# One spread table for the head norm weights and sinks, accumulating transfers kept away from the merge transposes, and new places for side work, in a hybrid attention/MLP step

## The chip, the cores and the metric

The kernel runs on one core of a Trainium2 chip. The metric is the time of one execution on the device, in microseconds (us): the median of the runs before is 1329.82 us (three runs, 1328.12 to 1332.52). One execution was also taken with the hardware profiler; its trace gives start, duration and cause of waiting of each instruction.

A core has five engines that each run their own list of instructions in order and wait for each other by semaphores: TensorE (PE in the profile, with PEld for its weight loads), VectorE (DVE), ScalarE (ACT), GpSimd (POOL) and SyncE (SP), which here only issues transfers (DMAs).

## The reference, cut to what matters

One trunk layer of a diffusion backbone, for 128 context tokens (`x_prompt`) and 128 latent tokens (`x_sample`), width 2048, all in float32:

```python
sh1, sc1, g1, sh2, sc2, g2 = split(silu(cond) @ w_ada + b_ada, 6)
h = rms_norm(x, norm1_w) * (1 + sc1) + sh1
qa, ka, va, qb, kb, vb, ga, gb = split(h @ w_in)        # 2048 x 8704
qa, ka = rms_norm(qa, q_norm_a), rms_norm(ka, k_norm_a) # per head of 128
qb, kb = rms_norm(qb, q_norm_b), rms_norm(kb, k_norm_b)
oa = windowed attention, 8 heads, 2 kv heads, a learned sink logit sink_a per head
ob = neighbourhood attention, 8 heads, relative position bias
x = x + g1 * ((sigmoid(ga) * (oa @ w_br_a) + sigmoid(gb) * (ob @ w_br_b)) @ w_out)
h2 = rms_norm(x, norm2_w) * (1 + sc2) + sh2
x = x + g2 * (relu(h2 @ w_up) ** 2 @ w_down)            # 2048 x 8192 x 2048
```

Latent tokens also get a rotary embedding and attend to cached context keys. The new context keys and values are outputs as well.

## The kernel before, in words

**Weight steps.** The 256 tokens are the stationary side of the matmuls and the weights stream past them. All weights come as tiles of 128 x 1024 floats (512 KB, `raw`). A float32 product is made of three fast ones: a tile is split into a rounded high half `wH` and a rest `wL`, the tokens likewise (`hH`, `hL`), and PE adds wH·hH, wL·hH and wH·hL into `acc`. One tile is one *weight step*: a load issued by SP (L220), a copy to `wH` by ACT (L98), a subtraction `wL` = `raw` − `wH` by DVE (L246), and twelve matmuls (L296 to L298, or L414 to L416 in the first projection). There are 456 such steps: 0 to 71 the first part of the input projection (nine units q, k, v, taken in chunks of the depth), 72 to 135 the eight gate units, 136 to 167 the two branches (`w_br_a`, `w_br_b`, four column units each), 168 to 199 `w_out`, and 200 to 455 the MLP in pieces of an up part and a down part. The up part forms some products from sums of two tiles (`XH`, `XL`, `YB`, `FAST`).

**The low half by transfer.** For the steps in the list `LO_DMA` DVE does not subtract. ACT writes −wH into `wL` (L252), and POOL issues a transfer that adds the weight tile to it in memory (L253, `accum_op`). Nineteen steps are on the list, among them 163, the last tile of the fourth `w_br_a` unit.

**Order.** The order is written by hand. `run()` goes through the steps; for step i it first issues the loads due up to step i + RUN[i], then prepares `wH` and `wL` up to step i + LOOK[i], then the step's matmuls, then the side work hung on that step (`at`). Each of RUN and LOOK is a string with a digit for each step. A name with `_AT`, `POST`, `JOBS`, `T_PAIR`, `P_PAIR`, `P_UP`, `T_UP`, `DOTS` is a table of the step, or the distance in steps, at which a piece of side work stands. An engine takes its instructions in that order, so one that waits holds up all that stand behind it on the same engine.

**Side work that the prediction names.**
- *Constants* (`load_consts`, loaded at the place CONST_AT[0], near step 68): the rotary table, three head norm weights of 128 floats each spread over the 128 partitions, the sink logits spread in the same way, and the cached keys and values. They go through SP's queue among the weight tiles. `load_bias` (CONST_AT[1]) loads the position bias, which POOL then masks with eight selects (L643, L645).
- *Head norm* (`POST`): ACT squares (L664), POOL raises to −1/2 (L141, L142), ACT and DVE apply it (L675 to L688).
- *Dots* (L1388, `DOTS1`, `DOTS`, `DOTS2`): the other part of the modulation is made on DVE, as row sums of `w_ada` tiles (`aT`) with silu(cond) (`cB`), 128 x 1024 at a time; the result goes to `aT` or to `junk` by turns. The first part is made on PE in pairs (`ps_ada`, L313).
- *Merge* (`br_unit`): the merged columns of unit n must be transposed to become the stationary side of `w_out`. For n = 0 to 2 this is done in three steps: `part` (ACT copies the halves of each float to 16-bit planes `plm`), `flip` (SP issues one transposing transfer, `pTm`, L871) and `join` (ACT puts the planes together as `fTm`, and ACT and DVE split it into `m0H`/`m0L` and so on). M_AT gives the distance of the three from the end of the unit. Unit 3 is transposed by PE (`ps_T`, L848). `h2f` and `ps_h` (L1029, L1037) are the second norm.

Of the kernel before, what the change touches and what calls it, by code (L numbers as in the profile page):

```python
# [18 lines left out]
P = 128  # L19
D = 2048  # L20
KC = D // P
HD = 128
NH = 8
# [9 lines left out]
FB_DVE = 2  # L33
FB1 = 14
H_AT = 38
DOTS1 = [11, 15, 23, 28, 29, 31, 33, 34]
CHUNKS = [2, 2, 2, 4, 6]
NFAST = 8
FAST = {1: (0, 3, 7), 2: (0, 2, 4, 6, 7), 3: (0, 2, 3, 4, 7), 4: (0, 2, 4, 6, 7), 5: (0, 1, 3, 4, 7), 6: (0, 1, 4, 5, 7), 7: (0, 3, 4, 6, 7)}
SEED_AT = 3  # L40
KEEP = True
ROWS_AT = [8, 6, 3]
SEED1_AT = 2
SEED1 = "101111011111111111001100111011111111"
# [7 lines left out]
LOOK = "234335453022344432223322221123343443443222223775666676366646455654435553343455556665357644436452334433332233221321432244644644245355400233120425355623477665676447546554534564644667674253021316344751443634211245334554433356554223123421445424543633220000235565775443654553304536544534445434543233444323223545687654344342323322202410232434423542333435554555523324223333334435433334435442300123332434534633245342656444443412231330344475554454323213432233345544"  # L52
RUN = "649522021012233424433334222110112541121112232345556555534334554224554454565572101322134333222224454542222001333311333323442545661430123142722355655565555757423433576442014141257765376943474743254236564587423656644454665553123312233345542334335654105653231354445553432211112222432232322202344422121133432312342242430331200000222233345444243334543434963332212101334433643322111332122223312234344436665443012022332200131013374556744346778788775545334442222234"
# [8 lines left out]
PREP_IN = [6, 8]  # L62
DOTS = [33, 41, 44, 44, 47, 47, 48, 50, 52, 52, 52, 55, 57, 57, 57, 58, 62, 67, 70, 70, 73, 75, 82, 84, 84, 88, 90, 92, 93, 94, 95, 99, 99, 99, 103, 103, 105, 105, 108, 108, 111, 112, 114, 114, 115, 118, 119, 120, 121, 121, 124, 124, 125, 128, 129, 132, 132, 132, 132, 134, 136, 138, 140, 143, 143, 144, 149, 150, 151, 151, 152, 157, 157, 163, 165, 169, 171, 171, 173, 175, 176, 176, 178, 179, 179, 183, 183, 190]
DOTS2 = [222, 231, 232, 233, 235, 237, 238, 242, 245, 263, 265, 269, 275, 299, 301, 301, 302, 329, 331, 333, 333, 334, 358, 360, 362, 364, 366, 368, 383, 391, 392, 396]
STAT_AT = [-1, -1, 9, 17]
T_PAIR = [[8, 10], [6, 8], [8, 8], [8, 10], [10, 14], [8, 10], [11, 14]]
P_PAIR = [[6, 6], [2, 2], [1, 4], [4, 2], [3, 2], [5, 2], [4, 4]]
M_TE = (3,)
M_AT = [4, 6, 9]
FLIP = 1  # L70
P_UP = [3, 0]
T_UP = [6, 8]
COL = {"qA": 0, "kvA": 1024, "qB": 1536, "kB": 2560, "vB": 3584, "gA": 4608, "gB": 6656}


# [1 line left out]
def tile_hybrid_step(ctx: ExitStack, tc: tile.TileContext, a):  # L77
# [8 lines left out]
    act, dve, pe, pool, sync = nc.scalar, nc.vector, nc.tensor, nc.gpsimd, nc.sync  # L86
# [179 lines left out]

    by_dma = sorted(LO_DMA)

# [335 lines left out]
    def load_consts():  # L604
        rc = G("rope")[:, 0:256].rearrange("p (a b c) -> p a b c", a=2, b=4)
        sync.dma_start(rc.rearrange("p a b c -> p (a b c)"), a["rope"])
        k2 = G("k2")
        wb = k2[:, 512:896].rearrange("p (n d) -> p n d", n=3)
        for n, name in enumerate(("q_norm_a", "k_norm_a", "k_norm_b")):
            sync.dma_start(wb[:, n, :], a[name][0].partition_broadcast(P))  # L610
        dve.tensor_scalar(wb, wb, float(HD) ** 0.5, None, op0=OP.mult)
        dve.tensor_scalar(qkw, qkw, float(HD) ** 0.5, None, op0=OP.mult)
        K2["wb"] = {"kvA": wb[:, 1, :], "kB": wb[:, 2, :]}

        for n, name in enumerate(("qA", "kvA")):
# [12 lines left out]
        sync.dma_start(ca[:, 1], a["cache_a_v"][0, 0])  # L628
        kT, cbv = (G(n).rearrange("p (h d) -> p h d", h=NH) for n in ("kTcB", "cbv"))
        sync.dma_start(kT, a["cache_b_kT"])  # L630
        sync.dma_start(cbv, a["cache_b_v"][0, 0])
        K2["ca"], K2["kTcA"], K2["kTcB"], K2["cbv"] = ca, ca[:, 0], kT, cbv
# [874 lines left out]
def _layout(x):  # L1507

    def tiles(w, n=512):
        k, m = w.shape  # L1510
        return w.reshape(k // 256, 2, P, m // n, n).transpose(0, 3, 2, 1, 4).reshape(k // 256, m // n, P, 2 * n)

    out = {n: x[n] for n in ("x_prompt", "x_sample", "b_ada", "q_norm_a", "k_norm_a", "q_norm_b", "k_norm_b", "sink_a",
                             "cache_a_v", "cache_b_v")}
# [53 lines left out]
```

## Time and profile before

| | |
|---|---|
| median of 3 runs | 1329.82 us |
| profiled execution, its own time | 1329.58 us |
| its span, first to last instruction | 1327.8 us |
| POOL's 19 transfers L253, issue to landing | 5.2 / 8.3 / 17.3 us (min, median, max) |
| copy to wH on ACT, L98 | 392.4 us in 393, 1044 ns each |
| subtraction wL on DVE, L246 | 436.3 us in 368, 1223 ns each |
| dots on DVE, L1388 | 154.9 us in 128 (`aT`) and 154.2 us in 128 (`junk`) |
| bytes moved | 390.68 MB, mean 294 GB/s |

In the rows of a timeline the first number is the start in us from the span's start, the second the duration; then engine, line, operation, output<-input and how many instructions the row groups. A bracket gives the idle time before and what ended it. A row of stretches gives, for each engine, its busy time (and number of instructions), then the clock that TensorE was granted, the DMA share and the GB/s. Matmuls overlap: one starts about every 0.227 us and is shown as 0.39 us long.

### The profile page before, as it was taken

Reading aid. Unit: us, or ns where it says so; the run is one execution under the profiler, and the core shown is the slowest. Engines: PE = TensorE matmul, PEld = TensorE weight load, DVE = VectorE, ACT = ScalarE, POOL = GpSimd, SP = SyncE. Lnnn points to the kernel's source line nnn. Section 1 sums busy time; section 2 is a strip of 40 time slices with the busy share of each in tenths; the row PEclk is TensorE's granted clock in tenths of the full one; section 3 lists DMA queues with packets and bytes.
Section 4 is the critical chain, followed back from the end, with each engine's and each line's share of the span. In section 5 each row is a group of like instructions: output and inputs, shape, how many; then the busy total and the mean of one; then the engine's idle time right before and its main releaser. Section 6 shows DMA issues by size and latency. Waiting matters only on the chain.

```text
span 1327.8 us, 17958 instructions
## 1 busy us (share of the span) xinstructions
PE 1309.4 (99%) x6275; PEld 1062.4 (80%) x6276; DVE 1117.6 (84%) x1476; ACT 911.6 (69%) x1284; POOL 57.3 (4%) x65
## 2 busy tenths in 40 slices
PE   8999999999999999899999999999999999999998
PEld 4777788788787888787888888888888888888887
DVE  4557899988899999799769989898989999969654
ACT  5777665787755565555687777968768687786871
POOL 0000003321000000000000000000000000000000
PEclk9999999999999999999999999999999999999999
DMA  9999996967699999999677995879676786976592
GB/s 375 408 409 409 408 390 214 397 217 271 208 398 398 404 374 277 303 378 355 200 253 270 283 274 203 270 230 293 234 293 218 253 277 235 312 205 246 174 359 95
DMA packets 147963, 390.68 MB, mean 294 GB/s; under 512 B 51872, under 2 KB 53088, under 8 KB 147872
## 3 DMA queue, kind: packets, MB, share of 16 engines
q1 hardware_dynamic: 144448, 378.16, 78.9%
q0 software_dynamic: 3280, 11.29, 4.7%
q8 instruction: 49, 0.80, 0.2%
q14 instruction: 42, 0.34, 0.1%
q10 hardware_dynamic: 144, 0.08, 0.0%
HBM read 370.83 MB, written 8.70 MB: 286 GB/s over the span
## 4 chain that ended last, share of the span: by engine, by line
PE 82%; DMA 6%; DVE 5%; issue 3%; ACT 2%; SPq 0%; POOL 0%; DVEq 0%; ACTq 0%; POOLq 0%
PE acc L297 14%; PE acc L298 14%; PE acc L296 14%; PE Q L1165 6%; PE Q L1164 6%; PE Q L1166 6%; PE acc L414 4%; PE acc L416 4%; PE acc L415 4%; DVE wL L246 3%; DMA araw<-in_w_pair 2%; PE ps_ada L313 2%; DMA wL<-in_w_br_a 1%; ACT wH L98 1%; DVE junk L1388 1%
## 5 line engine op out<-in xcount | busy, mean ns | idle before, releaser
L246 DVE TENSOR_TENSOR wL<-raw,wH 128x1024 fp32r<-128x1024 f32 x368 | 436.3, 1223 | 104.7 <-ACT wH L98 103.6
L98 ACT ACTIVATE wH<-raw 128x1024 fp32r<-128x1024 f32 (+1 forms) x393 | 392.4, 1044 | 50.8 <-DMA raw<-in_w_out 9.3
L1388 DVE SCALAR_TENSOR_TENSOR aT<-aT,cB 128x1024 f32<-128x1024 f32 x128 | 154.9, 1227 | 0.7
L1388 DVE SCALAR_TENSOR_TENSOR junk<-aT,cB 128x1024 bf16<-128x1024 f32 x128 | 154.2, 1221 | 0.4 <-ACT t L956 0.4
L414 PE MATMUL acc<-wH,hH 128*128 128x512 f32 x276 | 108.9, 394 | 0.0
L415 PE MATMUL acc<-wL,hH 128*128 128x512 f32 x276 | 107.6, 390 | 0.0
L416 PE MATMUL acc<-wH,hL 128*128 128x512 f32 x276 | 107.5, 390 | 0.0
L297 PE MATMUL acc<-wL,hH 128*128 128x512 f32 x256 | 100.0, 391 | 2.5 <-DVE wL L246 2.5
L296 PE MATMUL acc<-wH,hH 128*128 128x512 f32 x256 | 102.5, 400 | 0.0
L298 PE MATMUL acc<-wH,hL 128*128 128x512 f32 x256 | 99.9, 390 | 0.0
L98 ACT ACTIVATE uH<-raw 128x1024 fp32r<-128x1024 f32 x33 | 35.0, 1062 | 63.9 <-DVE raw L1226 62.1
L414 PEld LDWEIGHTS acc<-wH,hH 128*128 128x128 f32 x276 | 51.8, 188 | 13.2 <-issue 2.1
L416 PEld LDWEIGHTS acc<-wH,hL 128*128 128x128 f32 x276 | 51.8, 188 | 11.0
L415 PEld LDWEIGHTS acc<-wL,hH 128*128 128x128 f32 x276 | 51.8, 188 | 10.6 <-DVE wL L246 0.3
L297 PEld LDWEIGHTS acc<-wL,hH 128*128 128x128 f32 x256 | 48.2, 188 | 12.7 <-DVE wL L246 3.3
L296 PEld LDWEIGHTS acc<-wH,hH 128*128 128x128 f32 x256 | 48.1, 188 | 10.2 <-ACT prob L788 0.4
L298 PEld LDWEIGHTS acc<-wH,hL 128*128 128x128 f32 x256 | 48.1, 188 | 10.2
L98 ACT ACTIVATE tH<-t 128x1024 fp32r<-128x1024 f32 x33 | 35.0, 1060 | 29.9 <-DVE t L1219 26.3
L1229 DVE TENSOR_TENSOR uL<-raw,uH 128x1024 fp32r<-128x1024 f32 x33 | 40.4, 1225 | 1.2
L98 ACT ACTIVATE acc<-dsum 128x512 f32<-128x512 f32 x56 | 31.7, 590 | 13.7 <-DVE t L950 7.8
L98 ACT ACTIVATE fTa<-pTa 128x2048 uint16<-128x2048 uint16 x16 | 40.5, 2530 | 0.7 <-DMA pTa<-pla 0.7
L1228 DVE TENSOR_TENSOR tL<-t,tH 128x1024 fp32r<-128x1024 f32 x33 | 40.1, 1216 | 1.0 <-PE Z L1165 1.0
(644 smaller groups left out, 3200.7 us busy)
## 6 DMA issues: line engine op xcount, KB each, us to landing
raw<-in_w_in SPq DMA_DIRECT2D x133, 512.0 KB, 9.0
raw<-in_w_down SPq DMA_DIRECT2D x128, 512.0 KB, 6.3
raw<-in_w_upF SPq DMA_DIRECT2D x66, 512.0 KB, 4.8
araw<-in_w_pair SPq DMA_DIRECT2D x64, 512.0 KB, 10.2
aT<-in_w_adaT SPq DMA_DIRECT2D x64, 512.0 KB, 8.9
aT<-in_w_gT SPq DMA_DIRECT2D x64, 512.0 KB, 7.4
raw<-in_w_up SPq DMA_DIRECT2D x62, 512.0 KB, 5.2
raw<-in_w_out SPq DMA_DIRECT2D x32, 512.0 KB, 11.6
```

The source lines that it names most:

```text
L98: act.activation(out, in_, AF.Copy)
L246: dve.tensor_tensor(st["lo"], st["raw"], st["hi"].bitcast(F32), op=OP.subtract)
L296: pe.matmul(acc[tb], sh, wh[:, k, :], start=f, stop=False, skip_group_check=seeded)
L297: pe.matmul(acc[tb], sh, wl[:, k, :], start=False, stop=False, skip_group_check=seeded)
L298: pe.matmul(acc[tb], sl, wh[:, k, :], start=False, stop=l, skip_group_check=seeded)
L414: pe.matmul(acc[tb], sh, wh[:, k, :], start=opened[u] and k == 0, stop=False, skip_group_check=skip)
L415: pe.matmul(acc[tb], sh, wl[:, k, :], start=False, stop=False, skip_group_check=skip)
L416: pe.matmul(acc[tb], sl, wh[:, k, :], start=False, stop=last and k == 1, skip_group_check=skip)
L1164: pe.matmul(acc, stat[0], hi, start=f, stop=False)
L1165: pe.matmul(acc, stat[0], lo, start=False, stop=False)
L1166: pe.matmul(acc, stat[1], hi, start=False, stop=l)
L1388: dve.scalar_tensor_tensor(out, box["raw"], 1.0, cB[s, tag], op0=OP.mult, op1=OP.mult, accum_out=dst[:, s, fb:fb + 1])
```

## The change

The three head norm weights and the sinks are put into one array `heads` on the host (392 floats, repeated for 128 partitions, 200 KB) and come in one load in place of four. Steps 86 and 163 leave the LO_DMA list, so that DVE subtracts there, and 67, 330 and 363 join it, for which ACT and POOL do the work; an assertion keeps the list free of steps 148 to 173 (br0 is 136). M_AT starts the merge planes and their transposes earlier, and many entries of RUN, LOOK and the tables of side work are new. The changes in SEED1 leave the instructions as they were; FAST has as many fast products as before, in other places.

```diff
-DOTS1 = [11, 15, 23, 28, 29, 31, 33, 34]
+DOTS1 = [11, 17, 23, 28, 29, 31, 35, 35]
-FAST = {1: (0, 3, 7), 2: (0, 2, 4, 6, 7), 3: (0, 2, 3, 4, 7), 4: (0, 2, 4, 6, 7), 5: (0, 1, 3, 4, 7), 6: (0, 1, 4, 5, 7), 7: (0, 3, 4, 6, 7)}
+FAST = {1: (0, 5, 7), 2: (0, 2, 4, 6, 7), 3: (0, 2, 3, 4, 7), 4: (0, 2, 3, 4, 7), 5: (0, 1, 3, 4, 7), 6: (0, 1, 4, 5, 7), 7: (0, 3, 4, 6, 7)}
-BACK = 8
+BACK = 7
-GATE_BACK = 8
+GATE_BACK = 7
-LO_DMA = [86, 107, 129, 145, 163, 177, 184, 187, 189, 192, 236, 250, 254, 255, 297, 389, 392, 404, 436]
+LO_DMA = [67, 107, 129, 145, 177, 184, 187, 189, 192, 236, 250, 254, 255, 297, 330, 363, 389, 392, 404, 436]
-CONST_AT = [68, 64]
+CONST_AT = [68, 66]
-ADA_AT = [None, 4, 13, 18, 21, 38, 29]
+ADA_AT = [None, 4, 13, 18, 21, 38, 31]
-M_AT = [4, 6, 9]
+M_AT = [3, 4, 9]
...
@@ load_consts
         wb = k2[:, 512:896].rearrange("p (n d) -> p n d", n=3)
-        for n, name in enumerate(("q_norm_a", "k_norm_a", "k_norm_b")):
-            sync.dma_start(wb[:, n, :], a[name][0].partition_broadcast(P))
+        sync.dma_start(k2[:, 512:896 + NH], a["heads"])
...
-        sync.dma_start(sk[:, 0, :], a["sink_a"][0].partition_broadcast(P))
...
     br0 = len(wsteps)
+    assert not any(br0 + 12 <= j < br0 + 38 for j in LO_DMA)
...
@@ _layout
+    heads = np.concatenate([x[n].reshape(-1) for n in ("q_norm_a", "k_norm_a", "k_norm_b", "sink_a")])
+    out["heads"] = np.broadcast_to(heads, (P, 3 * HD + NH))
```

What this does to the order is seen best in three places. First SP's queue near step 68, where the constants stand among the weight tiles (the kernel before):

```order
L220 DMA raw<-in_w_in 128x1024 x3
L606 DMA rope<-in_rope 128x256
L610 DMA k_2276<-in_q_norm_a 128x128
L610 DMA k_2276<-in_k_norm_a 128x128
L610 DMA k_2276<-in_k_norm_b 128x128
L623 DMA k_2276<-in_sink_a 128x8
L627 DMA cacheA<-in_cache_a_kT 128x256
```

and the same place of the changed kernel, where the bias load stands too:

```order
L635 DMA bias<-in_rpb_qk 128x1024
L220 DMA raw<-in_w_in 128x1024 x2
L606 DMA rope<-in_rope 128x256
L609 DMA k_2277<-in_heads 128x392
L625 DMA cacheA<-in_cache_a_kT 128x256
```

Four small loads have become one, and the bias load has come closer to them, with two weight tiles between.

Second ACT's list around the second merge transpose (fTm is its result as ACT puts it together; L252 is the negated copy of step 163, L826 a gate's sigmoid), before:

```order
L98 ACTIVATE wH<-raw 128x1024
L98 ACTIVATE plm_5009<-g_gA_4509 128x1024 x2
L98 ACTIVATE wH<-raw 128x1024
L252 ACTIVATE wL<-wH 128x1024
L98 ACTIVATE wH<-raw 128x1024 x3
L826 ACTIVATE g_gB_4775<-g_gB_4775 128x1024
L98 ACTIVATE fTm_5112<-pTm_5059 128x2x1024
L98 ACTIVATE m1H<-fTm_5112 128x1024
L98 ACTIVATE wH<-raw 128x1024 x4
```

and of the changed kernel:

```order
L98 ACTIVATE wH<-raw 128x1024
L98 ACTIVATE plm_4987<-g_gA_4508 128x1024 x2
L98 ACTIVATE wH<-raw 128x1024 x5
L824 ACTIVATE g_gB_4791<-g_gB_4791 128x1024
L98 ACTIVATE fTm_5109<-pTm_5006 128x2x1024
L98 ACTIVATE m1H<-fTm_5109 128x1024
L98 ACTIVATE wH<-raw 128x1024 x3
```

The negated copy is gone, and the wH copy of one more step (165) stands ahead of fTm.

Third DVE's list ahead of the low half of step 181, around the first residual sum of `w_out` (t and x), before:

```order
L1388 SCALAR_TENSOR_TENSOR aT,half_4535<-aT,cB_3696 128x1024
L950 TENSOR_TENSOR t<-g_0_5177,acc 128x512 x2
L952 TENSOR_TENSOR x_0_4538<-x_0_4538,t 128x512 x2
L1388 SCALAR_TENSOR_TENSOR junk,half_4587<-aT,cB_3694 128x1024
L1388 SCALAR_TENSOR_TENSOR aT,half_4587<-aT,cB_3696 128x1024
L1388 SCALAR_TENSOR_TENSOR junk,half_4535<-aT,cB_3694 128x1024
L1388 SCALAR_TENSOR_TENSOR junk,half_4587<-aT,cB_3694 128x1024
L246 TENSOR_TENSOR wL<-raw,wH 128x1024 x3
```

and of the changed kernel:

```order
L1387 SCALAR_TENSOR_TENSOR aT,half_4542<-aT,cB_3693 128x1024
L1387 SCALAR_TENSOR_TENSOR junk,half_4590<-aT,cB_3691 128x1024
L1387 SCALAR_TENSOR_TENSOR junk,half_4542<-aT,cB_3691 128x1024
L949 TENSOR_TENSOR t<-g_0_5169,acc 128x512 x2
L951 TENSOR_TENSOR x_0_4545<-x_0_4545,t 128x512 x2
L1387 SCALAR_TENSOR_TENSOR aT,half_4590<-aT,cB_3693 128x1024
L1387 SCALAR_TENSOR_TENSOR aT,half_4542<-aT,cB_3693 128x1024
L1387 SCALAR_TENSOR_TENSOR junk,half_4590<-aT,cB_3691 128x1024
L1387 SCALAR_TENSOR_TENSOR aT,half_4590<-aT,cB_3693 128x1024
L1387 SCALAR_TENSOR_TENSOR junk,half_4542<-aT,cB_3691 128x1024
L1387 SCALAR_TENSOR_TENSOR junk,half_4590<-aT,cB_3691 128x1024
L246 TENSOR_TENSOR wL<-raw,wH 128x1024 x3
```

Both pieces begin right behind the low halves of steps 179 and 180, and the last row is that of 181 to 183. Five dots stood between; now there are nine, three ahead of the residual sum and six behind it. The other four stood ahead of steps 179 and 180 before.

More of the change, by code (lines that the diff above doesn't have):

```diff
@@ L43 @@
 SEED1_AT = 2
-SEED1 = "101111011111111111001100111011111111"
-BACK = 8
+SEED1 = "101111011101111111111100111011111111"
+BACK = 7
 AWAY = [('gA', 1), ('gB', 2), ('gB', 3), ('gA', 0), ('gB', 0), ('gA', 2)]
-GATE_BACK = 8
+GATE_BACK = 7
 DIRECT = (3,)
-LO_DMA = [86, 107, 129, 145, 163, 177, 184, 187, 189, 192, 236, 250, 254, 255, 297, 389, 392, 404, 436]
+LO_DMA = [67, 107, 129, 145, 177, 184, 187, 189, 192, 236, 250, 254, 255, 297, 330, 363, 389, 392, 404, 436]
 LO_AHEAD = 2
-LOOK = "234335453022344432223322221123343443443222223775666676366646455654435553343455556665357644436452334433332233221321432244644644245355400233120425355623477665676447546554534564644667674253021316344751443634211245334554433356554223123421445424543633220000235565775443654553304536544534445434543233444323223545687654344342323322202410232434423542333435554555523324223333334435433334435442300123332434534633245342656444443412231330344475554454323213432233345544"
@@ L53 @@
[L53 to L54 removed]
+LOOK = "003435353022344232233323121123244343443222223775666676366746456654545452243455556665357644436452334433332233221320432034644644155344400233121425465623477665686447335542534664644666674153010205332640443745321334123554433356554212012421444314543633220001335565775443654553305536544534445435654332334323223545687654344342323322202521343544423543433435554665523324323222434435433334434442302345532434534633245341556444443302331330343364454454323213543333345544"
@@ L55 @@
+RUN = "256423133014343646521012013111102542111112221345556555534335665335654454565472212333234333223323233542333112334422444423442545661440145364944455655565666867533433576442035252257754265833575723254358785687423556644454665563123311233345542334325655205653231354445674432201112222542232322202344422121144543323342242420331100000222233345333132224543334963223312101334433643322122432122223312234344436665332012133443310010012264557843225667688775546445663322234"
+CONST_AT = [68, 66]
 XL_DMA = []
-ADA_AT = [None, 4, 13, 18, 21, 38, 29]
+ADA_AT = [None, 4, 13, 18, 21, 38, 31]
@@ L61 @@
 T_AT = [4, 4]
[L62 to L67, printed above, removed]
+PREP_IN = [6, 7]
+DOTS = [33, 41, 44, 44, 47, 47, 48, 50, 52, 52, 52, 55, 57, 57, 57, 58, 62, 67, 70, 71, 73, 75, 82, 84, 84, 88, 90, 92, 93, 94, 95, 99, 99, 99, 103, 103, 105, 105, 108, 108, 111, 112, 114, 114, 115, 118, 119, 120, 121, 121, 124, 124, 126, 128, 129, 132, 132, 132, 132, 134, 136, 138, 140, 143, 143, 144, 149, 151, 151, 152, 157, 157, 162, 163, 165, 172, 173, 174, 174, 175, 176, 176, 178, 179, 179, 183, 183, 190]
+DOTS2 = [226, 230, 232, 233, 235, 237, 238, 242, 245, 263, 265, 269, 275, 299, 301, 301, 302, 329, 331, 333, 333, 334, 358, 360, 362, 364, 366, 368, 383, 391, 392, 396]
+STAT_AT = [-1, -1, 8, 17]
+T_PAIR = [[8, 9], [6, 8], [8, 9], [8, 10], [10, 14], [8, 10], [11, 14]]
+P_PAIR = [[4, 6], [2, 2], [1, 4], [6, 2], [4, 2], [5, 2], [4, 2]]
 M_TE = (3,)
-M_AT = [4, 6, 9]
+M_AT = [3, 4, 9]
 FLIP = 1
-P_UP = [3, 0]
-T_UP = [6, 8]
+P_UP = [2, 0]
+T_UP = [6, 11]
 COL = {"qA": 0, "kvA": 1024, "qB": 1536, "kB": 2560, "vB": 3584, "gA": 4608, "gB": 6656}
@@ L1511, in tiles @@
         return w.reshape(k // 256, 2, P, m // n, n).transpose(0, 3, 2, 1, 4).reshape(k // 256, m // n, P, 2 * n)
-    out = {n: x[n] for n in ("x_prompt", "x_sample", "b_ada", "q_norm_a", "k_norm_a", "q_norm_b", "k_norm_b", "sink_a",
-                             "cache_a_v", "cache_b_v")}
+    out = {n: x[n] for n in ("x_prompt", "x_sample", "cache_a_v", "cache_b_v")}
+    heads = np.concatenate([x[n].reshape(-1) for n in ("q_norm_a", "k_norm_a", "k_norm_b", "sink_a")])
+    out["heads"] = np.broadcast_to(heads, (P, 3 * HD + NH))
     for n in ("w_in", "w_br_a", "w_br_b", "w_out", "w_up", "w_down"):
```

## The prediction

> **What bounds the kernel now.** I read the busy shares of the page first, then the table of what each engine waited for, then the stretches around the waits.
>
> ```profile
> PE 1309.4 (99%) x6275; PEld 1062.4 (80%) x6276; DVE 1117.6 (84%) x1476; ACT 911.6 (69%) x1284; POOL 57.3 (4%) x65
> ```
>
> TensorE (PE) is busy for 99% of the span. The change leaves its matmuls as they are, so it can gain only where PE waits or runs slowly. The table of PE's waits has (us in total, times, longest):
>
> ```profile
> PE acc L297 <- DMA wL<-in_w_br_a: 2.8, 1, 2.8
> PE acc L297 <- DVE wL L246: 2.5, 2, 1.8
> ...
> PE acc L1002 <- DMA wL<-in_w_out: 1.0, 1, 1.0
> PE ps_T L848 <- DVE g_gA L903: 0.7, 1, 0.7
> PE ps_h L1037 <- DVE h2f L1029: 0.7, 1, 0.7
> ```
>
> These five rows are 7.7 us; the rest of the table lies in the first 42 us, whose loads the change leaves in order. The first row is one stall, and PE's timeline there shows a second loss behind it (start, duration):
>
> ```profile
> 534.89 0.39 PE L298 MATMUL acc<-wH,oLA 128*128 128x512 f32 x1
> 535.11 0.39 PE L296 MATMUL acc<-wH,oHA 128*128 128x512 f32 x1
> 538.26 0.50 PE L297 MATMUL acc<-wL,oHA 128*128 128x512 f32 x1 [2.76 <-DMA wL<-in_w_br_a]
> ...
> 539.12 0.63 PE L297 MATMUL acc<-wL,oHA 128*128 128x512 f32 x1
> ...
> 542.49 0.39 PE L296 MATMUL acc<-wH,oHB 128*128 128x512 f32 x1
> ```
>
> Before the stall a matmul starts every 0.22 us. From 539.12 to 542.49 eight starts take 3.37 us, 0.42 each: 8 x 0.20 = 1.6 us lost after the pause. So this place costs 2.8 + 1.6 = **4.4 us**.
>
> Its cause: step 163 has its low half wL made by an accumulating transfer that POOL issues, and SP's transpose of merge plane 1 is under way at that time.
>
> ```profile
> 518.30 7.96 SPq L871 DMA_TRANSPOSE pTm<-plm  x1
> ```
> ```profile
> 520.88 0.85 POOL L253 DMA_DIRECT2D wL<-in_w_br_a  x1 [48.24 <-DVE aT L1388]
> ```
>
> The summary of each tile gives the time from issue to landing (min/median/max), for all 19 accumulating transfers and then for the three transposes:
>
> ```profile
> DMA to landing us min/median/max: 5.2/8.3/17.3
> ```
> ```profile
> DMA to landing us min/median/max: 10.3/11.0/20.6
> ```
>
> The maxima are this pair: 520.88 + 17.3 = 538.2, where PE resumes, and 518.30 + 20.6 = 538.9, where ACT resumes below. While both are open nearly nothing moves, though the DMA engines are marked busy (last two columns: DMA share, GB/s):
>
> ```profile
> 525.00:530.00 5.00, 5.00 (x24) 4.14 (x23) 5.00 (x7) 0.00 (x0) 0.00 (x0) 1.00 1.37 66
> 530.00:535.00 5.00, 5.00 (x24) 4.15 (x23) 5.00 (x9) 0.00 (x0) 0.00 (x0) 1.00 1.08 72
> ```
>
> ACT and DVE wait for the same transpose, and behind ACT's wait stand the next steps' wH copies:
>
> ```profile
> 519.53 1.06 ACT L252 ACTIVATE wL<-wH 128x1024 fp32r<-128x1024 f32 x1
> ...
> 538.94 2.51 ACT L98 ACTIVATE fTm<-pTm 128x2048 uint16<-128x2048 uint16 x1 [14.55 <-DMA pTm<-plm]
> ...
> 542.44 3.89 ACT L98 ACTIVATE wH<-raw 128x1024 fp32r<-128x1024 f32 x4
> ```
> ```profile
> 542.57 1.22 DVE L102 TENSOR_TENSOR m1L<-fTm,m1H 128x1024 fp32r<-128x1024 f32 x1 [5.51 <-ACT m1H L98]
> 543.71 4.62 DVE L246 TENSOR_TENSOR wL<-raw,wH 128x1024 fp32r<-128x1024 f32 x4
> ```
>
> **The change, part by part.** (a) *Step 163 leaves the DMA list.* DVE gets a subtraction (4.62 / 4 = 1.16 us), ACT loses a copy of 1.06 us, POOL a transfer. The transpose should then take what the other two took, 10.3 to 11.0 us, and land near 529; ACT resumes some 9 us earlier. DVE's new 1.16 us come out of its 5.51 us of idle time, and the wL of 163 to 165 stand ahead of m1L now. I take the whole -4.4. The bounds are -4.4 and -3.0. The -3.0 is if the transpose still lands at 538.9: wL.166 ends two subtractions behind 542.57, at 544.9, and PE, which would want it three steps (36 x 0.227 = 8.2 us) behind 535.3, at 543.5, waits 1.4 us there.
>
> The Trainium skill speaks against this step: "DMA: Bandwidth & Descriptors", section "Rules for kernel authors", has "A transpose next to ordinary DMAs needs nothing". By that the transpose would be as late without the accumulation, and (a) would be its small end; the trace has 20.6 us beside the accumulation against 10.3 and 11.0 without, so I weigh it as the weaker.
>
> (b) *Merge planes one step earlier; the merge transpose no longer late.* The ps_T wait at 560 is for DVE's merge sums. DVE gains 5.51 - 1.16 = 4.35 us, PE 4.4, so it nearly stays; with the dots moved around it I take -0.3 (bounds -0.7 and 0).
>
> (c) *One load for norm weights and sinks.* Stretches before (DMA share, GB/s last):
>
> ```profile
> 227.00:232.00 5.00, 5.00 (x24) 4.14 (x23) 5.00 (x7) 1.20 (x2) 2.56 (x2) 1.00 0.15 33
> ...
> 236.00:240.00 4.00, 4.00 (x20) 3.30 (x19) 4.00 (x9) 3.33 (x11) 2.32 (x2) 1.00 1.03 406
> ```
>
> While the four broadcasts are served the queue moves 33 GB/s instead of 406, for about 5 us. One 200 KB load at 406 GB/s is 0.5 us (an estimate from that row), so the weights behind it land about 4.5 us earlier. Who waits for them:
>
> ```profile
> 241.96 1.06 ACT L98 ACTIVATE wH<-raw 128x1024 fp32r<-128x1024 f32 x1 [2.64 <-DMA raw<-in_w_in]
> 242.93 1.07 ACT L98 ACTIVATE u_vB<-acc 128x512 f32<-128x512 f32 x2
> ```
>
> That wait starts the chain to the 2.5 us row: ACT's squares, POOL's power, DVE's query block, two dots, then wL.76:
>
> ```profile
> 249.88 2.48 POOL L142 TENSOR_TENSOR rq<-rs,pw 128x8 f32<-128x8 f32 x1
> ```
> ```profile
> 252.39 0.69 DVE L676 TENSOR_TENSOR u_qA<-u_qA,rq 128x512 f32<-128x512 f32 x1 [0.41 <-POOL rq L142]
> ...
> 255.25 1.22 DVE L1388 SCALAR_TENSOR_TENSOR aT<-aT,cB 128x1024 f32<-128x1024 f32 x1
> ...
> 257.96 2.36 DVE L246 TENSOR_TENSOR wL<-raw,wH 128x1024 fp32r<-128x1024 f32 x2 [0.34 <-ACT wH L98]
> ```
> ```profile
> 259.24 0.51 PE L297 MATMUL acc<-wL,hH 128*128 128x512 f32 x1 [0.76 <-DVE wL L246]
> ...
> 266.76 0.51 PE L297 MATMUL acc<-wL,hH 128*128 128x512 f32 x1 [1.78 <-DVE wL L246]
> ```
>
> The 2.64 us go, but u_vB waits for PE's own sum, whose last matmul is
>
> ```profile
> 240.83 0.39 PE L416 MATMUL acc<-wH,hL 128*128 128x512 f32 x1
> ```
>
> and ends at 241.2. So the chain moves by 242.93 - 241.2 = 1.7 us at most; I take 1.4, since a wH copy can stand in the way. A dot (1.2 us, the 255.25 row) that stood before the query block now follows it, ahead of wL.76. Net: wL.76 some 0.6 us earlier, and the 0.76 nearly goes. At the second place DVE and PE both come 0.6 earlier, and 1.78 stays. I take **-0.6**; the bounds are -2.5 (all goes) and +1.2 (chain unmoved, dot added).
>
> (d) *Late w_out stalls (1.0 and some tenths).* DVE is the pacer there; two of its idle times wait for wH behind accumulating steps whose raw had just landed:
>
> ```profile
> 591.91 2.36 DVE L246 TENSOR_TENSOR wL<-raw,wH 128x1024 fp32r<-128x1024 f32 x2 [0.96 <-ACT wH L98]
> ...
> 598.32 2.36 DVE L246 TENSOR_TENSOR wL<-raw,wH 128x1024 fp32r<-128x1024 f32 x2 [0.61 <-ACT wH L98]
> ```
>
> With the transfer queue 9 us earlier behind the transpose and PE only 4.4, these 1.6 us go: **-1.0** (bounds -1.4; +1.2, if the added subtraction shows instead). (e) The ps_h wait of 0.7 grows as PE comes earlier than DVE: +0.4 (0 to +1.1).
>
> (f) *The rest*: dots, fast positions, pair 6, bias load, steps 67, 330 and 363 on the DMA list in place of 86 and 163, all move work inside stages where PE waits for nothing in the table. Nearest in margin is the block of step 252, where XL ends at 787.27 and PE takes it at 787.94:
>
> ```profile
> 786.05 1.22 DVE L1225 TENSOR_TENSOR XL<-raw,XH 128x1024 fp32r<-128x1024 f32 x1
> ```
> ```profile
> 787.94 0.39 PE L1165 MATMUL Q<-XL,h20H 128*128 128x512 f32 x1
> ```
>
> Until step 330 DVE carries one subtraction more (1.16 against this 0.67). DVE's earlier idle times hide it, so 0; without that cover +0.5.
>
> The sum: -4.4 - 0.3 - 0.6 - 1.0 + 0.4 = -5.9 on the profiled execution's 1329.58 us (span 1327.8 and 1.8 around it), 1323.7. That execution lies 0.24 under the median of 1329.82, so **1323.9**, by itself 1321.5 to 1325.5.
>
> **Rivals.**
> *B, the heads load frees both stalls at 259 and 267.* For it: the 1.78 is behind the same POOL power step. Against: the added dot. (c) is -2.5: 1322.0.
> *C, DVE eats the gain.* PE comes 4.4 us earlier into w_out, DVE 4.35 at most; if the subtraction of step 163 is not hidden, (d) is +1.2 rather than -1.0: 1326.1. For it: DVE is the pacer from 565 to 625.
> *T, the transpose is slow by itself.* (a) -3.0, (d) 0, DVE gaining about 1 us on 3: +1.9 at step 181; -3.0 + 1.9 - 0.3 - 0.6 = -2.0: 1327.8.
> *D, the single load is no faster than the broadcasts.* Then (c) is +1.2 and the time 1325.7. Against it: 33 GB/s at a share of 0.15 is a queue that waits, and rows of the raw loads run at 406. The Trainium skill ("DMA: Bandwidth & Descriptors", section "Specifications") puts the least transfer for line rate at 512 B, which the broadcast rows have already; by that alone nothing would be won, and the 33 GB/s row disagrees for this pattern.
> *A, slower: VectorE becomes the bound of the dense stage.* If DVE gains no time by 252, its timeline of before plus 1.16 less the 0.67 of margin sets the end: +0.5 on 1329.82, 1330.3. It decides once DVE regains less than 0.5 us of its idle time before 780. Against it stand the 5.51 us alone.
>
> **How the numbers follow.** The forecast 0.48, C 0.17, B 0.10, T 0.10, D 0.08, A 0.07. Predicted is the likeliest, 1323.9. The low end is every term's good bound but (a), near 1320.5; the high end takes in C, D, T and comes up to A, 1330.0. A measurement of this kernel can tell about 0.3% (4.0 us) from no change: faster is under 1325.8. That is the forecast, B, and a part of D and C: 0.72. Over 1333.8 lies only a case of A that is worse than priced: 0.04. The rest, 0.24, is the same.
>
> **What would show it.** (a): no wait for wL<-in_w_br_a, the pTm maximum near 11 us, no 0.42 us pitch near 540. (b), (e): the ps_T and ps_h rows. (c): GB/s near 400 within 2 us of the heads load, a wait of about 1.9 us for wL L246 near 265. (d): no L1002 row. Wrong it would be if the pTm maximum stays near 20 us, or if new rows for wL L246 appear behind 650.

## The result and the profile after

| | before | after |
|---|---|---|
| median | 1329.49 us (4 runs, 1328.12 to 1332.52) | 1319.99 us (4 runs, 1319.65 to 1320.42) |
| profiled execution, its own time | 1329.58 us | 1319.65 us |
| span | 1327.8 us | 1317.9 us |

The ratio is 0.9926 (0.9908 to 0.9943): the kernel became 9.5 us faster, by the profiled executions 9.9. Forecast were 5.9, and 1320.5 as the low end, so the time came 0.5 us below the range. The places were the right ones; three terms were too small, and one had the wrong sign.

The busy shares of the changed kernel, the same row as before:

```profile
PE 1305.9 (99%) x6275; PEld 1061.6 (81%) x6276; DVE 1116.6 (85%) x1475; ACT 912.5 (69%) x1285; POOL 57.2 (4%) x66
```

Each engine has the work of before, within 4 us; the span is 9.9 shorter, so waiting and slow matmuls went. PE's waits after (us in total, times, longest):

```profile
PE ps_ada L313 <- DMA araw<-in_w_pair: 2.3, 4, 0.6
PE acc L499 <- ACT hH L98: 1.3, 2, 0.9
PE ps_warm L123 <- DVE pro L116: 1.2, 1, 1.2
PE acc L297 <- DVE wL L246: 1.0, 1, 1.0
```

Of the five rows of before one is left, with 1.0 instead of 2.5; all others that the table has lie in the first 42 us. No wait for `wL<-in_w_br_a`, `in_w_out`, ps_T or ps_h is in the table. The summaries of the accumulating transfers and of the three transposes, issue to landing (min/median/max):

```profile
DMA to landing us min/median/max: 5.4/8.2/10.3
```
```profile
DMA to landing us min/median/max: 9.0/9.2/10.3
```

The maxima of 17.3 and 20.6 are gone. The transpose that took 20.6 is now issued at 516.16, and ACT puts its result together at 525.46 instead of 538.94; DVE, which stood idle for 5.51 before m1L, stands idle there no more. Rows of SP, ACT and DVE:

```profile
516.16 7.25 SPq L869 DMA_TRANSPOSE pTm<-plm  x1
```
```profile
525.46 2.55 ACT L98 ACTIVATE fTm<-pTm 128x2048 uint16<-128x2048 uint16 x1 [1.99 <-DMA pTm<-plm]
```
```profile
535.01 1.22 DVE L102 TENSOR_TENSOR m1L<-fTm,m1H 128x1024 fp32r<-128x1024 f32 x1
```

In the stretches that moved 66 and 72 GB/s before, the DMAs now move (last column):

```profile
525.00:530.00 5.00, 5.00 (x23) 4.13 (x22) 5.00 (x6) 4.51 (x4) 0.00 (x0) 1.00 0.93 289
530.00:535.00 5.00, 5.00 (x23) 4.13 (x22) 4.93 (x10) 2.07 (x3) 0.00 (x0) 1.00 1.03 415
```

And the stretch near step 68, 33 GB/s before:

```profile
227.00:232.00 5.00, 5.00 (x24) 4.13 (x23) 5.00 (x6) 1.20 (x2) 4.88 (x4) 1.00 1.05 409
```

To see where the time went I paired PE's matmuls of the two traces, which are the same in the same order, and took the start of the first wH matmul of a step (us, and after less before):

| step | before | after | difference |
|---|---|---|---|
| 66 | 230.2 | 230.0 | −0.2 |
| 79 | 270.2 | 267.9 | −2.3 |
| 163 | 535.1 | 533.2 | −1.9 |
| 164 | 542.5 | 535.9 | −6.6 |
| 171 | 563.5 | 556.1 | −7.4 |
| 192 | 621.4 | 613.2 | −8.2 |
| 194 | 625.4 | 615.9 | −9.5 |
| 201 | 648.4 | 638.5 | −10.0 |
| 455 | 1318.9 | 1308.8 | −10.1 |

Between two rows of the table stands what one place gave: the heads load −2.1 by step 79 (0.25 of it is lost again by step 94), step 163 −4.65, the ps_T wait −0.81, three places in `w_out` together −1.86 (at 181, 184 and 192), the ps_h wait −0.55. Behind step 201 nothing changes.

### The profile page after: what moved, and what is told of

Its sections match the earlier page's. It is cut to its first block, busy times and chain, and to the rows that moved or that the text cites. A ratio compares the mean times of both kernels' runs of the same rounds, so it can differ in the third digit from the quotient of the medians.

```text
span 1317.9 us, 17969 instructions
## 1 busy us (share of the span) xinstructions
PE 1305.9 (99%) x6275; PEld 1061.6 (81%) x6276; DVE 1116.6 (85%) x1475; ACT 912.5 (69%) x1285; POOL 57.2 (4%) x66
## 4 chain that ended last, share of the span: by engine, by line
PE 96%; DMA 3%; ACT 1%; DVE 0%; SPq 0%; issue 0%; DVEq 0%; ACTq 0%
PE acc L297 17%; PE acc L298 17%; PE acc L296 17%; PE Q L1165 6%; PE Q L1164 6%; PE Q L1163 6%; PE acc L414 5%; PE acc L416 5%; PE acc L415 5%; DMA araw<-in_w_pair 2%; PE ps_ada L313 2%; PE ps_S L746 1%; PE Z L1165 1%; PE Z L1164 1%; PE Z L1163 1%; PE acc L1001 1%
## 5 line engine op out<-in xcount | busy, mean ns | idle before, releaser
L246 DVE TENSOR_TENSOR wL<-raw,wH 128x1024 fp32r<-128x1024 f32 x367 | 434.0, 1222 | 92.9 <-ACT wH L98 90.0
L1218 DVE TENSOR_TENSOR t<-raw 128x1024 f32<-128x1024 f32 x33 | 40.2, 1218 | 1.6 <-PE Q L1164 1.6
L98 ACT ACTIVATE dsum<-acc 128x512 f32<-128x512 f32 x56 | 31.2, 588 | 14.0 <-PE acc L298 13.0
```

The costliest lines, as they stand in the source:

```text
L98: act.activation(out, in_, AF.Copy)
L246: dve.tensor_tensor(st["lo"], st["raw"], st["hi"].bitcast(F32), op=OP.subtract)
```

## The experiments

Four things had to be told apart: which of the edits carries the gain, what makes the transpose late, what made the four small loads slow, and what the rest of the wait near step 78 is worth. Every ratio below is to the kernel before on the same chip.

**Which edit carries it.** First the changed kernel once more, the reference for the runs beside it.

> The changed kernel once more, as the yardstick for the runs beside it: 1319.5 to 1320.5, POOL's power step for the first query unit at about 246.8, one wait of about 1.0 us for wL at step 78.

1320.23 us (6 runs, 1319.49 to 1321.43), ratio 0.9942 (0.9919 to 0.9964).

Then the changed kernel with one number put back, and the assertion left out:

```diff
-LO_DMA = [67, 107, 129, 145, 177, ...
+LO_DMA = [67, 107, 129, 145, 163, 177, ...
```

> The changed kernel with step 163 back on the list of accumulating transfers, all else as changed. Theory M (the accumulation and the merge transpose hold each other up, and most of what follows in w_out is DVE's idle time from that): the transfer takes 15 us or more, the second transpose 17 us or more, a stall of 2 to 4 us at step 163 comes back, and with it waits at the merge and in w_out; 1325 to 1327. Rival P (the new places did it: the merge planes now stand a step earlier, so the transpose is nearly through when the transfer starts): both land within 12 us and the time stays within 1 us of the changed kernel, 1319.5 to 1321.

1330.1 us (11 runs, 1328.12 to 1331.43), ratio 1.0007 (0.9995 to 1.0019): the whole gain is undone, which is more than theory M had (1327 at most). Rival P falls: both transfers are late in the new places too. PE's waits, then the summaries of the accumulating transfers and of the transposes, and one stretch:

```profile
PE acc L297 <- DMA wL<-in_w_br_a: 3.4, 1, 3.4
...
PE ps_T L846 <- DVE g_gA L901: 2.0, 2, 1.3
```
```profile
DMA to landing us min/median/max: 5.4/8.3/18.5
```
```profile
DMA to landing us min/median/max: 10.5/11.6/21.0
```
```profile
525.00:530.00 5.00, 5.00 (x24) 4.14 (x23) 5.00 (x7) 0.00 (x0) 0.00 (x0) 1.00 1.40 64
...
558.00:563.00 5.00, 4.30 (x15) 3.55 (x15) 5.00 (x5) 4.70 (x5) 0.00 (x0) 0.66 1.04 413
```

The pair of 18.5 and 21.0 is back with all its marks, and it costs more than the stall: step 164 comes 3.7 us later than in the changed kernel, step 171 7.4 and step 455 8.5. The added part lies at the ps_T wait (2.0), behind which TensorE's granted clock is 0.66 for 5 us in this execution.

The other way round, the kernel before with 163 taken off the list and nothing else:

```diff
-LO_DMA = [86, 107, 129, 145, 163, 177, ...
+LO_DMA = [86, 107, 129, 145, 177, ...
```

> The kernel before with one number taken out: step 163 leaves the list. Theory M: the transpose lands 10 to 11 us after issue, the 4.4 us at step 163 go, and so do 0.5 to 2 us of waits behind it (the merge at 560, the late low halves of steps 184 and 192), since DVE gets back 5.5 + 1.6 us of idle time for one subtraction; 1329.5 - 4.6 - 1.5 = 1323.4, between 1322.5 and 1325. Rival P: without the new places a stall of 1 to 3 us comes back at step 166 and behind it; 1326 to 1328. Rival T (the transpose is slow by itself): it still lands about 20 us after issue; 1327 to 1329.

1323.62 us (6 runs, 1321.82 to 1325.88), ratio 0.9956 (0.9939 to 0.9972). By the paired starts the profiled execution gains 4.65 at step 163 and 2.7 more by step 201. It ends only 3.7 us earlier than the kernel before, because it had lost 3.6 by step 94, where its granted clock was 0.68 (42 to 46 us) and 0.72 (268 to 274 us); it is the slowest of its six runs. The medians say 5.4. Transfers, transposes, and a stretch in which the transpose is open alone:

```profile
DMA to landing us min/median/max: 5.3/8.1/10.4
```
```profile
DMA to landing us min/median/max: 9.0/9.8/11.8
```
```profile
525.00:530.00 5.00, 5.00 (x24) 4.14 (x23) 5.00 (x9) 2.01 (x2) 0.00 (x0) 1.00 1.21 252
```

One step off the list cures the transpose, without the earlier merge planes; the stalls of `w_out` go with it.

The heads load alone, in the kernel before (its lines as in the diff of the change):

> The kernel before with the single load of the head norm weights and sinks, all else as before. If the single load is what moved the chain to steps 76 and 78: the raw tile behind the constants lands some 4 us earlier, POOL's power step for the first query unit starts at about 246.8 in place of 249.88, the waits at 259 and 267 fall from 2.5 to 1 us or less; 1327.3 to 1328.2. If the new place of the bias load and of the dots did it: POOL's step moves by less than 1 us and the time stays within 0.7 us of the kernel before.

1326.93 us (12 runs, 1319.6 to 1331.64), ratio 0.9981 (0.9967 to 0.9995), some 2.5 us, with a wide spread of runs. Waits for wL L246 near steps 76 to 78 are 1.2 in all instead of 2.5. So it is in the other traces: with the four broadcasts at the old places (before, e2, e4, e9) these waits are 2.0 to 2.6 in all, with the table 1.0 to 1.3. The paired starts are less sure there: e4 and e9 come 1.2 and 0.7 us earlier from step 66 to 79 than the kernel before, with the same loads. In its profiled execution the pair at 163 took 14.9 and 18.2 us.

Both edits, without any of the new tables:

> The kernel before with two edits only: step 163 off the list, and the single load of norm weights and sinks. No place of side work is new. If these two carry the whole change: the stall at 163 and the late low half of step 192 go (4.65 + 1.2 + about 1 in the stages behind), and of the waits at 259 and 267 some 1.3 to 2 us; 1320.0 to 1322.0. If the new places carry a part that shows: 1322.5 to 1325.

1320.78 us (6 runs, 1320.22 to 1322.82), ratio 0.9938 (0.9920 to 0.9956). The two gains add (0.0044 + 0.0019 against 0.0062), and they are the change: the interval lies on that of the changed kernel. Of the new tables the trace shows the ps_T wait, 0.9 here and none after; in the time they cannot be seen.

```profile
PE ps_T L846 <- DVE g_gA L901: 0.9, 2, 0.7
```

**What makes the transpose late.** In the kernel before, the transfer of step 163 without the addition, so that the low half of that step is the whole tile:

```diff
+        if st["i"] == 163:
+            act.activation(st["lo"], st["hi"].bitcast(F32), AF.Copy, scale=-1.0)
+            pool.dma_start(st["lo"], st["src"].bitcast(F32R))
+        else:
+            minus_plus(st["lo"], st["hi"], st["src"])
```

> The kernel before, with the transfer of step 163 without its addition: POOL still issues the same 512 KB from memory into the same tile at the same place, but it overwrites (the low half of this step is then the whole tile). It tells apart accumulation from any transfer that POOL issues. If the accumulation (which reads its destination too) is what the transpose does not go along with: the transfer lands within 9 us, the transpose within 12, no stall at step 163; 1323 to 1325.5. If any transfer issued by POOL beside a transpose is enough: 15 us or more for the one, 18 or more for the other, and 1328.5 to 1330.5.

1325.39 us (11 runs, 1323.19 to 1329.34), ratio 0.9977 (0.9964 to 0.9990), between before and e2. Transfers, transposes, and the stretches in which both are open:

```profile
DMA to landing us min/median/max: 5.4/8.2/13.9
```
```profile
DMA to landing us min/median/max: 10.0/11.5/16.7
```
```profile
522.00:527.00 5.00, 5.00 (x23) 4.14 (x23) 5.00 (x7) 1.20 (x2) 0.00 (x0) 1.00 1.40 124
527.00:532.00 5.00, 5.00 (x23) 4.13 (x23) 5.00 (x9) 0.00 (x0) 0.00 (x0) 1.00 1.10 125
```

A plain transfer also stretches the transpose, to 16.7 us, and is stretched itself; the addition makes it worse. Whether that is POOL's queue, the next run asks: the kernel of e2 with one more 512 KB load that nobody reads, issued by ACT inside the transpose.

```diff
+    at(157, lambda: act.dma_start(G("extra"), wsteps[163]["src"]))
```

> The kernel before with step 163 off the list, and one load more: 512 KB of weights, issued by ACT right behind its wH copies while SP's second transpose is under way, into a tile that nobody reads. It asks whether any transfer that starts inside a transpose holds it up, or one that POOL issues. If POOL's way of issuing is the cause: the load lands within 9 us, the transpose within 12, and the time is within 1 us of the kernel with step 163 alone off the list, 1322.5 to 1324.5. If any transfer will do: the transpose takes 15 us or more and the load 12 or more; 1324 to 1327.

1323.9 us (8 runs, 1322.49 to 1324.99), ratio 0.9959 (0.9944 to 0.9973). The transposes, the extra load and the stretches:

```profile
DMA to landing us min/median/max: 9.9/11.3/16.0
```
```profile
DMA to landing us min/median/max: 12.3/12.3/12.3
```
```profile
522.00:527.00 5.00, 5.00 (x23) 4.13 (x22) 5.00 (x8) 0.87 (x1) 0.00 (x0) 1.00 1.34 143
527.00:532.00 5.00, 5.00 (x24) 4.14 (x23) 5.00 (x6) 0.00 (x0) 0.00 (x0) 1.00 1.03 143
```

So it is neither POOL nor the addition alone: a 512 KB load that starts inside a transpose is slow (12.3 us, against a median of 8.2 for the accumulating ones of this run) and makes the transpose slow, whether POOL or ACT issues it. PE has slack for a transpose of 16 us here, which is why the time stays that of e2; a wait of 1.5 for `in_w_out` comes back.

Then the same collision made at another plane, in the changed kernel: step 154 put on the list, whose transfer falls into the first transpose.

> The changed kernel with step 154 added to the list, so that its accumulating transfer starts some 3 us into the first merge transpose. It asks whether the second transpose was special. Theory M: the first transpose takes 15 us or more in place of 10.3, the transfer 13 or more, ACT puts the first plane together 5 us later; PE, which has some 6 us of lead there, waits 0 to 2 us at most; 1320 to 1323. If only the second place was special: both land within 12 us, and the time is within 0.7 us of the changed kernel.

1326.7 us (12 runs, 1323.67 to 1329.07), ratio 0.9984 (0.9971 to 0.9997): some 6.5 us above the changed kernel. Transfers, transposes, a stretch, and PE's waits:

```profile
DMA to landing us min/median/max: 5.4/8.5/16.5
```
```profile
DMA to landing us min/median/max: 11.3/12.3/20.1
```
```profile
505.00:510.00 5.00, 5.00 (x23) 4.13 (x23) 0.64 (x1) 0.00 (x0) 0.00 (x0) 1.00 1.21 75
```
```profile
PE acc L296 <- DVE g_gB L900: 2.1, 4, 1.3
PE ps_T L846 <- DVE g_gA L901: 1.9, 2, 1.2
...
PE acc L296 <- DVE g_gA L894: 1.2, 1, 1.2
```

The mechanism is not one of step 163. PE never waits for this transfer. ACT waits 12.2 us for a weight tile that SP loads (`in_w_br_b`, up to 512.2 us) and DVE 7.6 us behind ACT (the 0.64 us of DVE in 5); their arrears reach PE at the sums of the gates, from 516 to 542 us, and at ps_T, at 559. The cost was larger than expected (1320 to 1323).

**What made the small loads slow.** First in the changed kernel, with its new places: the four broadcasts back; one load of 1568 B rows, all 128 from the same place; four loads of 512 B rows from the spread table.

```diff
-        sync.dma_start(k2[:, 512:896 + NH], a["heads"])
+        sync.dma_start(wb[:, n, :], a[name][0].partition_broadcast(P))             # e5, n = 0 to 2, and sinks
+        sync.dma_start(k2[:, 512:896 + NH], a["heads"].partition_broadcast(P))     # e6
+        sync.dma_start(wb[:, n, :], a["heads"][:, n * HD:(n + 1) * HD])            # e7, n = 0 to 2, and sinks
```

> The changed kernel with the four small loads (three broadcasts of 64 KB and the sinks) in place of the one, all else as changed. If the form of the load made the gain at steps 76 to 78: 28 to 40 GB/s for about 5 us behind the rotary table, the weights behind it 4 us or more later, 1.5 to 2.5 us of waits more; 1321.5 to 1322.5. If the new places hide it by now: within 0.5 us of the yardstick.

1320.17 us (8 runs, 1319.39 to 1322.22), ratio 0.9936 (0.9916 to 0.9957).

> The changed kernel with one load of 392 floats that all 128 partitions read from one place in memory (1568 bytes each), in place of the spread table. It tells what was slow: the same bytes of memory being read 128 times, or rows of 512 bytes and four loads. If reading one place is slow: the load takes 4 us or more to land behind the table and the time is as with four loads, 1321 to 1322.5. If the rows' length or the number of loads is: it lands within 2 us of the rotary table, and the time is within 0.5 us of the yardstick.

1320.39 us (9 runs, 1319.48 to 1321.47), ratio 0.9943 (0.9924 to 0.9961).

> The changed kernel with the spread table read by four loads (rows of 512 bytes, and 32 for the sinks) in place of one. The other half of the same question. If reading one place is slow: the four land within 2 us of the rotary table and the time is within 0.5 us of the yardstick. If rows of 512 bytes or four loads are slow: 4 us or more, and 1321 to 1322.5.

1319.57 us (5 runs, 1318.25 to 1319.92), ratio 0.9928 (0.9903 to 0.9953).

The time tells none of the four ways from another. In the trace e5 is 0.9 us late at step 79, with a wait of 1.8 in place of 1.0, and stays so, which the medians cannot show; at the old places the medians of e2 and e8 lie 2.8 apart. So the new places seem to hide a part of the broadcasts; how much is not shown, since e4 and e9, at the old places, have waits of 2.0 and 2.1. The stretches do tell the loads apart (e5, e6, e7):

```profile
227.00:232.00 5.00, 5.00 (x24) 4.14 (x23) 5.00 (x6) 1.20 (x2) 4.84 (x4) 1.00 0.53 141
```
```profile
227.00:232.00 5.00, 5.00 (x24) 4.14 (x23) 5.00 (x5) 1.20 (x2) 4.82 (x5) 1.00 1.05 407
```
```profile
227.00:232.00 5.00, 5.00 (x24) 4.14 (x23) 5.00 (x5) 1.20 (x2) 4.88 (x4) 1.00 0.87 302
```

Since the new places may cover the loads, e6 and e7 were asked again in the kernel of e8, which has the old places.

> The kernel before with step 163 off the list and one load of 392 floats that all partitions read from one place (rows of 1568 bytes), no new places. Beside the kernel with the spread table, 1320.8, and that with the four broadcasts, 1323.6. If rows of 512 bytes read from one place are the slow form, this one is not: 300 GB/s or more behind the rotary table, 1320.2 to 1321.5. If reading one place is slow by itself: 150 GB/s or less, 1322.5 to 1324.

1321.16 us (5 runs, 1320.83 to 1321.4), ratio 0.9944 (0.9931 to 0.9958).

> The kernel before with step 163 off the list and the spread table read by four loads (rows of 512 bytes), no new places. If the short rows are slow only from one place: 250 GB/s or more, 1320.2 to 1321.5. If rows of 512 bytes or the count of loads are slow by themselves: 150 GB/s or less, 1322.5 to 1324.

1320.59 us (5 runs, 1320.36 to 1321.82), ratio 0.9943 (0.9930 to 0.9955). Both medians are as e8's; the intervals overlap that of e2 (0.9956, with the broadcasts at the old places), so the times alone decide nothing. The waits for wL L246 do, 1.2 and 1.0 in all against 2.6 in e2, and so do the stretches of e13 (less than the 300 GB/s it was to reach) and e14, beside 33 GB/s of before:

```profile
227.00:232.00 5.00, 5.00 (x23) 4.13 (x22) 5.00 (x5) 1.20 (x2) 3.28 (x3) 1.00 0.82 264
```
```profile
227.00:232.00 5.00, 5.00 (x24) 4.14 (x23) 5.00 (x7) 1.20 (x2) 1.66 (x2) 1.00 0.90 257
```

Slow are only the four broadcasts, rows of 512 B (32 B for the sinks) that are each read 128 times from one place. One load of longer rows from one place is not slow, nor are four loads of the short rows spread out; so neither the number of loads nor the broadcast alone is the cause. Which of the two it takes beside the broadcast, short rows or several loads, is not shown: e6 and e13 changed both at once. The Trainium skill ("DMA: Bandwidth & Descriptors", section "Specifications") asks for 512 B; e14's rows of that size run well, and the broadcasts of before, with the same rows, do not.

**The rest of the wait near step 78.** First a dot moved from step 75 to 78 in the changed kernel.

```diff
-DOTS = [..., 70, 71, 73, 75, 82, 84, ...
+DOTS = [..., 70, 71, 73, 78, 82, 84, ...
```

> The changed kernel with one dot pair moved from step 75 to step 78, behind the second query unit's norm. It takes two dots (2.3 us) out of DVE's list ahead of the low half of step 78, where PE waits 1.0 us, and where POOL's power step is done 3 us before DVE begins the block. If that wait is DVE's order: it goes, with nothing in its place, 1318.7 to 1319.5. If ACT's copy of step 78 or POOL sets it: within 0.5 us of the changed kernel.

1319.87 us (6 runs, 1319.37 to 1321.46), ratio 0.9929 (0.9909 to 0.9948). The wait of 1.1 stayed: the dots moved had stood behind the low halves of 78 and 79 already, so this run answers nothing. Then those that do stand ahead of them:

```diff
-DOTS = [..., 70, 71, 73, 75, 82, 84, ...
+DOTS = [..., 70, 71, 76, 76, 82, 84, ...
```

> The changed kernel with the two dots that stand between the low half of step 77 and the second query unit's block moved behind that block (places 73 and 75 of the table both to 76). If DVE's order ahead of the low half of step 78 makes the last wait of 1.0 us: it goes, 318.7 less than a thousand times... that is 1318.7 to 1319.4. If ACT's copy of step 78 or POOL's power step sets it: within 0.4 us of the changed kernel.

(The time meant in it is 1318.7.) 1319.92 us (5 runs, 1319.42 to 1320.09), ratio 0.9935 (0.9922 to 0.9947). The wait near 78 is gone, and from step 66 PE comes 1.33 us earlier to step 79 than in the changed kernel; by step 91 it has given back 1.21. One of PE's waits is new, in the attention:

```profile
PE ps_PT L793 <- ACT prob L786: 0.6, 1, 0.6
```

Taking away PE's last wait there hands it to ACT's attention chain: no gain, and no version of these beat the changed kernel by more than the measurement's interval.

## Why the prediction was wrong, and where it was right

The places, the direction and most causes were right; the time fell below the range. The step that failed is the one from which (d), (e) and rival C were worked out, that DVE gains 4.35 us and PE 4.4, so that PE comes earlier than DVE. The runs show that DVE gains 6.1 us and is ahead of PE, by 1.7 us in e2. Besides, (b) and (c) were priced too small.

**(a) Step 163, forecast −4.4, measured −4.65.** Right, and for its reason: e1 and e2 move the stall with one number, and the landing of both transfers with it. The small end, −3.0, supposed a transpose still late; it came 13.5 us earlier (525.46 against 538.94). Rival T falls with it. The slow matmuls behind the stall belong to a low granted clock, 0.60 in the row below, and are not tied to the stall as firmly: in e1, behind a stall of 3.4, matmuls start every 0.23 us, and the slow stretch comes 20 us later.

```profile
538.26:542.49 4.23, 4.23 (x12) 3.34 (x13) 0.00 (x0) 3.52 (x3) 0.00 (x0) 0.60 1.04 387
```

But the cause was put too narrowly. e9's 16.0 and e4's 16.7 beside plain transfers, against 9.0 to 11.8 in e2, show the stretching without accumulation; beside accumulation it was 18.2 to 21.0. The sentence of the Trainium skill quoted in the prediction stands beside the rule that two transposes from different queues must wait for each other because they corrupt each other's data. It says nothing of time, so it did not speak against this step; how long a transpose takes next to an ordinary load, these two runs show.

**(b) ps_T, −0.3 against −0.81.** For step 163 alone "it nearly stays" is right: in e2 and e8 the ps_T wait is 0.9 us, 0.2 more than before. Mis-sized was "the dots moved around it", the −0.3. The merge sum that ps_T waits for starts 1.2 us earlier in the changed kernel than in e8, and PE only 0.2 (step 164 at 535.9 and 536.1), so the wait goes. DVE in e8, then in the changed kernel:

```profile
553.26 0.69 DVE L901 TENSOR_TENSOR g_gA<-g_gA,g_gB 128x512 f32<-128x512 f32 x1
```
```profile
552.05 0.69 DVE L901 TENSOR_TENSOR g_gA<-g_gA,g_gB 128x512 f32<-128x512 f32 x1
```

Which of the new tables moves it was not tried.

**(d) `w_out`, −1.0 against −1.86; (e) ps_h, +0.4 against −0.55.** Here "DVE gains 5.51 - 1.16 = 4.35 us, PE 4.4" fails. It left out a second idle time of DVE, behind the merge sums, that hung on the same late transpose: ACT's copies for the third plane stood behind its join of the second, so the third plane was late too. DVE before:

```profile
564.04 1.22 DVE L102 TENSOR_TENSOR m2L<-fTm,m2H 128x1024 fp32r<-128x1024 f32 x1 [1.60 <-ACT m2H L98]
```

and after:

```profile
553.79 2.35 DVE L246 TENSOR_TENSOR wL<-raw,wH 128x1024 fp32r<-128x1024 f32 x2
556.06 1.22 DVE L102 TENSOR_TENSOR m2L<-fTm,m2H 128x1024 fp32r<-128x1024 f32 x1
```

m2L comes 7.98 us earlier. Of that 1.9 is what PE had gained by step 163, so DVE gains 6.1 here, near 5.51 + 1.60 − 1.16 = 5.95; in e2, without the new places, it is 6.15, reckoned from step 163 in the same way. PE has gained 4.5 there in e2, so DVE is 1.7 us ahead of it; in the changed kernel, where PE has the gain at ps_T as well, 0.5. The idle times of 0.96 and 0.61 go besides: (d) let them go, and (e) did not count them. With DVE ahead, the stalls at steps 181 and 184 (0.63 together) and 192 (1.23) and the ps_h wait shrink instead of growing. The stall at 192 is one for a transfer, but it hangs on DVE as well: ACT makes the negated copy of 192 behind its wait for DVE's residual sum, and POOL issues the transfer 9.35 us earlier (613.05 to 603.70), where PE had gained 8.2. Rival C had the opposite; e2 and e8 speak against it, each with 2.7 us gained behind step 164.

**(c) The heads load, −0.6 against −2.0 at steps 76 to 78.** The step that failed here is "The 2.64 us go, but u_vB waits for PE's own sum", with the matmul at 240.83 as its last. That one belongs to step 69; the sum of the first u_vB was complete with step 68, whose last matmul after the change is the first of these rows (of PE, ACT, POOL, DVE and PE again):

```profile
237.88 0.39 PE L416 MATMUL acc<-wH,hL 128*128 128x512 f32 x1
```
```profile
239.16 1.05 ACT L98 ACTIVATE u_vB<-acc 128x512 f32<-128x512 f32 x2
```
```profile
246.79 2.47 POOL L142 TENSOR_TENSOR rq<-rs,pw 128x8 f32<-128x8 f32 x1
```
```profile
255.71 2.35 DVE L246 TENSOR_TENSOR wL<-raw,wH 128x1024 fp32r<-128x1024 f32 x2
```
```profile
264.51 0.50 PE L297 MATMUL acc<-wL,hH 128*128 128x512 f32 x1 [1.04 <-DVE wL L246]
```

It ends at 238.3. u_vB starts 3.8 us earlier than before (242.93 to 239.16), behind two wH copies and while step 69 still runs; POOL's power 3.1 (249.88 to 246.79), not the 1.4 assumed. The added dot takes part of it, and wL.76 comes 2.25 earlier (257.96 to 255.71). The 0.76 goes, as forecast; the 1.78 becomes 1.04, not the 1.9 that was to stay. This lies near rival B, which had both waits go (−2.5). Rival D falls by 409 GB/s. That the load does it, without the new places, e3 shows with 1.2 us for both waits. The −2.0 is of this one pair of executions: the waits alone give 1.5, the medians of e2 and e8, on different chips, 2.8.

**(f) The rest, forecast 0.** Right: PE's lead is 10.0 us at step 201 and 10.1 at the end, and e8 and the changed kernel take the same time. Rival A falls: PE waits nowhere for DVE behind step 201.

In sum −2.0 − 4.65 − 0.81 − 1.86 − 0.55 is −9.9 (the −0.2 up to step 66 and the 0.25 lost by 94 cancel), where −0.6 − 4.4 − 0.3 − 1.0 + 0.4 was forecast. The good bounds of the terms add up to −4.4 − 0.7 − 2.5 − 1.4 + 0 = −9.0, so 1320.8 and not the 1320.5 of the prediction. (c) stayed inside its bound; what took the time below the range is (d) and (e), which stood 0.46 and 0.55 us too high even at their bounds, with 0.25 of (a) and 0.11 of (b).

## What to carry to other kernels

When a late transfer goes, follow every engine that waited for it to its second wait, and add up all idle time that hangs on it; the engine that gains more than the bound one turns later stalls into gains. Start no large transfer inside a DMA transpose where an engine waits for either, and compare the longest landing time of both groups with the median: about twice the median was the mark here. For the wait of a copy on a sum, pair the copy with the matmul that really closes its accumulator, not with the last one of the stage.

## What the runs showed of the hardware that was not expected

- A transpose and a load that share time move little, though the DMA share is 1 or more: 64 to 90 GB/s beside an accumulating transfer, 124 to 143 beside a plain one, against 252 with the transpose alone (e2).
- The scatter of the executions goes with TensorE's granted clock. The 77 runs of the kernel before beside the experiments lie between 1323.98 and 1333.45 us; their medians are 1325.4 at a mean granted clock of 1.000, 1327.0 at 0.999, 1328.0 at 0.998, 1329.2 at 0.997 and 1331.0 at 0.996. The changed kernel scatters by 0.8 us in its 4 runs and by 1.9 in a0's 6, at 0.998 to 1.000; e3, with the late pair, by 12.0, at 0.996 to 1.000. What lowers the clock is not settled: it fell behind the stall at step 163, but in e2 also at 42 us, where PE's waits are those of before.
- The four small broadcasts hold the queue at 33 GB/s for about 5 us, at a DMA share of 0.15. They land 1.5 to 2.0 us apart (228.2, 229.7, 231.7 and 233.4 us), the sinks of 4 KB taking as long as the loads of 64 KB. What waits there the runs do not show.
